# Hybrid decoder step: operand making for the block products spread over steps and slots, a second plain set, decode columns in pairs, squares over PSUM

## The chip, the cores and the metric

The kernel runs on one core of a Trainium2 chip. The metric is the device time of one execution in microseconds (us). Before is the kernel as it stood, after is the changed one.

## The reference

The program is one inference step of a two-layer decoder with a prompt of 1024 tokens and 8 decode tokens, model width 1024, all in float32. Layer 0 is retention (4 heads, keys 256 wide, values 512 wide, chunks of 128 tokens), layer 1 is attention over a sliding window of 128. What matters here is layer 0, cut to its core:

```
h = rmsnorm(x, g_norm);  q, k, v, gate = split(h @ w_in)
# for each chunk c and head:
inner = (q_c @ k_c.T) * dmask
o_c   = inner @ v_c + (q_c @ S) * cross_decay
S     = S * chunk_decay + (k_c * k_decay).T @ v_c
# then:
o = rmsnorm(o, g_out) * silu(gate)
x1 = x + o @ w_out            # 2048 x 1024: "retention's projection"
```

Layer 1 starts with rmsnorm(x1), so the sums of squares of x1 (acc) are wanted too.

## The kernel before

**Split operands.** Every large matmul is made of float32 numbers split in two: hi is the number rounded (a cast, mostly on ACT), lo is what is left (a subtraction on DVE or POOL), and hi.hi + hi.lo + lo.hi are three matmuls. So each operand costs a cast and a subtraction before PE can use it.

**Block products.** The projections use a Winograd form: a 2x2 by 2x2 block product in seven products instead of eight (SEQ7, L316): A11.B11, S2.T2, S1.T1, A12.B21, S3.T3, S4.B22, A22.T4. A and S are weights and their sums, B and T are the data (heads and token parities) and its differences. `XH[t][x]`, `XL[t][x]` are the cells in which hi and lo of operand x lie, for each half t of the tokens; the cells are in the tiles SA and SB. T1 = B12 - B11, T2 = B22 - T1, T3 = T2 - B11, T4 = B21 - T2. Each cell has 256 columns of prompt tokens and 2 of decode tokens (`dec_cols`).

**The steps.** After the input projection come 32 steps of the recurrence, two heads in turn, first heads 0 and 1, then 2 and 3. In step i PE does `b_qk` of step i+1 (scores and the transposes of k), `b_mm` of step i (state S and output po), and `b_tr` of step i-1 (the transposes tr of the normed output on). The function `others` (L1057) gives the order on the other engines: og of step i-2 (DVE, L1055: tr times gate), Sh (ACT) and Sl (DVE, L1023), the sum of squares (ACT) with its scaling ts (DVE, L1034), the power pw on POOL (rsq, L119), the conversions of step i+1 (CONV, L827: sT, qh, vh, kh, kl, sh, vl, sl, ql), and on (ACT, L1042) after the first four of these. og is sent by DMA into the cells of heads 0 and 1, or, for heads 2 and 3, to DRAM (osc).

**Operand making in the steps.** Heads 0 and 1 are done halfway. From then on `x_items` (L1073) makes their operands: for each of four blocks (t, and a half c2 of its tokens) four differences on DVE (L1078, `do`) into temporaries `tm` in G0, seven casts on ACT, and seven subtractions (L1083) on POOL or, for each third, on DVE. The items form a list; three, at each fifth step four, are taken per step, and what is left is done at slot 1 of the projection. The first temporary of a block is also that of the next.

**The projection.** Eight sets (PSet, L1112), n = 0 to 7: phase P = n // 4 is heads 0 and 1 or heads 2 and 3, a = n % 4 a quarter of the output columns. A set has 14 slots of 12 matmuls (`p_prod`), or, in the plain form, 8 slots of 24 (`p_plain`, eight plain block products from B11, B21, B12, B22). Sets of phase one store partial sums to DRAM (pscr), which phase two loads and adds. `p_evac` (L1184) takes products out of PSUM, `p_pre` (L1197) adds partial results, `p_fin` (L1234) finishes x1: square into M01 (ACT, L1246) and add to acc (L1247), a store to xscr, and in set 7 the hi and lo of x1 for layer 1. `p_hi`, `p_lo` (L1166), `p_sum` make the weights' operands in tiles w, s1a, s2a, rb, ra.

**Operands of heads 2 and 3** are made during sets 3 to 5 by `split`, `t_sums` (y and z are their temporaries) and `dec_cols`, which overwrite the cells of heads 0 and 1 once these are read for the last time. Set 4 is plain, since it needs no T operands. In set 7 `a_load` and `a_split` (L1344, L1345) bring x1 of the first six column blocks back as the next layer's operand, and `kv_conv` splits weights of layer 1.

**What sets the order.** PE, ACT, DVE, POOL and SP all work through their own queue in program order, and that order is written by hand: `later(n, fn)` puts fn behind slot n, `when(time, fn)` puts it at a planned time, `others` and the items are put after each step. `p_plan` lists all of it for the sets. An engine that waits at the head of its queue holds everything behind it.

The lines that the prediction speaks of: L991 to L1004 `b_mm`, L104 transposes, L119 power, L300 `dec_on` (on of the decode tokens), L813 vl, L819 qh, L825 ql, L969 and L970 `dec_cols`, L1042 on, L1055 og, L1078 differences and casts of x_items, L1083 their subtractions, L1166 `p_lo`, L1195 evacuations, L1229 transposes of x, L1321 subtractions of `split`, L334 to L336 the matmuls of a product.

Of the kernel before, what the change touches and what calls it, by code (L numbers as in the profile page):

```python
# [70 lines left out]
def _trunk(ctx, tc, nc, a):  # L71
# [743 lines left out]
    def b_qh(h, c):  # L815
        d = heads[h]
        if c > 0:
            d["qh", c] = qt[0][h % 2]
            dve.tensor_copy(d["qh", c], d["l", c][0][:, 0:2, :])  # L819
# [220 lines left out]
    def b_on(h, c):  # L1040
        d = heads[h]
        act(d["on", c], d.pop(("po", c)), AF.Copy, scale=d["ss", c])  # L1042
# [28 lines left out]
    def x_items(t, c2):  # L1071
        cs = slice(128 * c2, 128 * c2 + 128)
        r = {x: raw_of(x, t)[:, :, cs] for x in (B11, B21, B22, T1)}  # L1073
        tm = [G0[:, 512 * j:512 * j + 512].rearrange("p (k f) -> p k f", k=4) for j in range(3)]
        its = []

        def do(fn, *a):
            its.append(lambda: fn(*a))  # L1078

        def parts(x, src):  # L1080
            n = len(its)
            do(act, XH[t][x][:, :, cs], src, AF.Copy)
            do(lambda: (pool if n % 3 else dve).tensor_tensor(XL[t][x][:, :, cs], src, XH[t][x].bitcast(F32)[:, :, cs], SUB))  # L1083
# [113 lines left out]
    def p_pre(s, t):  # L1197
        pool.tensor_tensor(s.c["w"][:, t], s.c["w"][:, t], s.c["x"][:, t], ADD)
# [35 lines left out]
    acc_on = set()  # L1234

    def p_fin(s, key, t):
        i, par = KEY[key]
        ft = 2 * s.a + i
        x1 = s.c[key][:, t, 0:256].rearrange("p (c y) -> p c y", c=2)
        gk = gcol[:, 16 + ft:17 + ft]  # L1240
        if s.n == 7:
            act(toks(A_hi[:, ft], t, par), x1, AF.Copy, scale=gk)
            dve.scalar_tensor_tensor(toks(A_lo[:, ft], t, par), x1, gk, toks(A_hif[:, ft], t, par), MUL, SUB)
        if (par, t) in acc_on:
            sq = M01[:, 0:256].rearrange("p (c y) -> p c y", c=2)
            act(sq, x1, AF.Square)  # L1246
            (pool if s.n == 7 else dve).tensor_tensor(toks(acc, t, par), toks(acc, t, par), sq, ADD)  # L1247
# [30 lines left out]
    def p_plain(s, par, i, t):  # L1278
# [18 lines left out]
        later(n + 1, p_fin, s, key, t)  # L1297
# [20 lines left out]
    def part(x, t, h, src, eng):  # L1318
        hi, lo = cells(x, t, h)
        act(hi, src, AF.Copy)  # L1320
        eng.tensor_tensor(lo, src, hi.bitcast(F32), SUB)  # L1321
# [1015 lines left out]
```

## Time and profile before

| what | us |
|---|---|
| median of 3 runs (1357.2 to 1361.32) | 1357.76 |
| profiled execution | 1358.83 |
| its span | 1357.0 |
| steps 5 to 31 of the recurrence | 560.09 to 702.49 |
| sets 0 to 7 of the projection | 702.49 to 917.30 |
| set 4, the plain one | 799.40 to 828.35 |

The times of the stages are from the start of the span, cut where PE starts each set's first matmul. Of a group of instructions the profile gives the line, engine, operation, tiles out<-in with shapes and count, then busy us and mean ns of one, then the idle time of the engine just ahead of them and what ended it. PE is busy 94% of the span, but a PE that is busy at a granted clock of 0.5 does half the work, so the clock has to be read beside it.

### The profile page before, as it was taken

The page shows a single profiled execution, that of the slowest core. Times are in us where ns is not written, and L with a number is a line of the kernel's source. Part 1 is how long each engine was busy: PE and PEld are TensorE (multiplying, and loading weights), DVE is VectorE, ACT ScalarE, POOL GpSimd, SP SyncE. Part 2 cuts the span into 40 slices and gives each one's busy share as a digit, 9 for nine tenths or more (in the row PEclk, how much of TensorE's full clock was granted, in tenths as well). Part 3 has the DMA queues.
Part 4 walks back from the last instruction along what each step waited for, and adds up shares of the span by engine and source line. Part 5 has one row for each costly group of instructions (what it writes and reads, how often), then busy time and mean ns, then how long its engine had stood idle before and what let it go on. Part 6 is the DMA issues. An engine that isn't in the chain of part 4 may idle for free.

```text
span 1357.0 us, 26895 instructions
## 1 busy us (share of the span) xinstructions
PE 1277.7 (94%) x9743; PEld 1216.5 (90%) x9743; DVE 822.9 (61%) x1590; ACT 693.6 (51%) x1664; POOL 812.6 (60%) x994
## 2 busy tenths in 40 slices
PE   6999999999999999888888986979998999999998
PEld 6999999999999999767778986879998999998998
DVE  6944656565666753688755589764565666766321
ACT  5532544545455644777761243355566666656221
POOL 6753534445389997687865667866567675645000
PEclk9999999999999999999999997989999999999999
DMA  6314677677757744768646672553113120218332
GB/s 220 103 63 151 212 241 214 200 214 204 248 162 230 218 147 139 216 187 264 214 142 173 183 267 88 140 160 105 55 52 101 40 86 32 95 47 270 95 95 80
DMA packets 230322, 208.79 MB, mean 154 GB/s; under 512 B 32889, under 2 KB 206197, under 8 KB 230173
## 3 DMA queue, kind: packets, MB, share of 16 engines
q1 hardware_dynamic: 198192, 172.71, 42.4%
q10 hardware_dynamic: 31996, 34.36, 7.8%
q8 instruction: 77, 1.26, 0.4%
q14 instruction: 57, 0.46, 0.1%
HBM read 134.36 MB, written 69.50 MB: 150 GB/s over the span
## 4 chain that ended last, share of the span: by engine, by line
PE 70%; DVE 8%; POOL 7%; ACT 5%; issue 5%; DMA 4%; SPq 1%; ACTq 0%; DVEq 0%; POOLq 0%
PE b L334 7%; PE b L335 7%; PE b L336 7%; PE pj L1607 5%; PE pj L1608 5%; PE pj L1609 5%; PE b L327 4%; PE b L328 4%; PE b L329 4%; PE tr L104 3%; PE b L543 2%; PE S L336 2%; PE S L334 1%; PE S L335 1%; PE o L1970 1%
## 5 line engine op out<-in xcount | busy, mean ns | idle before, releaser
L334 PE MATMUL b<-xh,woh 128*128 128x258 f32 x784 | 223.2, 285 | 0.0
L336 PE MATMUL b<-xh,wol 128*128 128x258 f32 x784 | 221.7, 283 | 0.0
L335 PE MATMUL b<-xl,woh 128*128 128x258 f32 x784 | 221.6, 283 | 0.0
L1607 PE MATMUL pj<-SA,wh 128*128 128x384 f32 (+1 forms) x512 | 174.7, 341 | 2.3 <-ACT SA L1990 1.3
L1608 PE MATMUL pj<-SA,wh 128*128 128x384 f32 (+1 forms) x512 | 164.3, 321 | 0.2 <-DVE SA L1991 0.2
L1609 PE MATMUL pj<-SA,wl 128*128 128x384 f32 (+1 forms) x512 | 164.5, 321 | 0.0
L334 PEld LDWEIGHTS b<-xh,woh 128*128 128x128 f32 x784 | 148.0, 189 | 4.1 <-issue 3.7
L335 PEld LDWEIGHTS b<-xl,woh 128*128 128x128 f32 x784 | 148.7, 190 | 0.0
L336 PEld LDWEIGHTS b<-xh,wol 128*128 128x128 f32 x784 | 148.0, 189 | 0.0
L225 POOL TENSOR_TENSOR wol<-raw,woh 128x512 fp32r<-128x512 f32 x52 | 68.0, 1318 | 119.7 <-ACT woh L220 108.6
L327 PE MATMUL b<-woh,xh 128*128 128x256 f32 x448 | 126.6, 283 | 0.0
L328 PE MATMUL b<-wol,xh 128*128 128x256 f32 x448 | 126.0, 281 | 0.0
L329 PE MATMUL b<-woh,xl 128*128 128x256 f32 x448 | 125.6, 280 | 0.0
L1607 PEld LDWEIGHTS pj<-SA,wh 128*128 128x128 f32 x512 | 96.7, 189 | 6.5 <-issue 2.6
L1608 PEld LDWEIGHTS pj<-SA,wh 128*128 128x128 f32 x512 | 96.9, 189 | 0.4 <-DVE SA L1991 0.4
L1609 PEld LDWEIGHTS pj<-SA,wl 128*128 128x128 f32 x512 | 96.5, 188 | 0.0
L1948 POOL TENSOR_TENSOR s<-s,sm 128x512 f32<-128x512 f32 x64 | 66.6, 1040 | 48.9 <-DVE sm L1947 44.6
L327 PEld LDWEIGHTS b<-woh,xh 128*128 128x128 f32 x448 | 84.3, 188 | 5.0 <-issue 2.9
L329 PEld LDWEIGHTS b<-woh,xl 128*128 128x128 f32 x448 | 84.3, 188 | 0.0
L328 PEld LDWEIGHTS b<-wol,xh 128*128 128x128 f32 x448 | 84.3, 188 | 0.0
L1940 ACT ACTIVATE s<-s,mx 128x257 f32<-128x257 f32 x128 | 64.2, 505 | 38.2 <-DVE mx L1938 37.3
L220 ACT ACTIVATE woh<-s 128x512 fp32r<-128x512 f32 x88 | 54.1, 624 | 53.3 <-POOL s L210 20.6
(544 smaller groups left out, 3927.3 us busy)
## 6 DMA issues: line engine op xcount, KB each, us to landing
raw<-in_w_in_ret_dram ACTq DMA_DIRECT2D x44, 512.0 KB
st<-in_state_ret_dram SPq DMA_DIRECT2D x64, 256.0 KB
out_dram<-st SPq DMA_DIRECT2D x64, 256.0 KB
vb<-vscr SPq DMA_DIRECT2D x64, 128.0 KB
evp<-qks SPq DMA_DIRECT2D x32, 256.0 KB
evx<-vsc SPq DMA_DIRECT2D x32, 256.0 KB
wr<-in_w_in_swa_dram SPq DMA_DIRECT2D x32, 256.0 KB
evc<-gsc SPq DMA_DIRECT2D x16, 256.0 KB
```

Source lines behind the costliest of these rows:

```text
L225: eng.tensor_tensor(lo, src_of(s, name, sub), hi.bitcast(F32), SUB)
L327: mm(dst, xh, wh, start=a and i == 0, stop=False, skip_group_check=True)
L328: mm(dst, xh, wl, start=False, stop=False, skip_group_check=True)
L329: mm(dst, xl, wh, start=False, stop=z, skip_group_check=True)
L334: mm(dst, wh, xh, start=a, stop=False, **sg)
L335: mm(dst, wh, xl, start=False, stop=False, **sg)
L336: mm(dst, wl, xh, start=False, stop=z, **sg)
L1607: mm(ps, hi[:, k, fs], xh[:, k, t0:t1], start=first and k == ks[0], stop=False)
L1608: mm(ps, hi[:, k, fs], xl[:, k, t0:t1], start=False, stop=False)
L1609: mm(ps, lo[:, k, fs], xh[:, k, t0:t1], start=False, stop=last and k == ks[-1])
L1940: nc.scalar.activation(st[:, j, :], st[:, j, :], AF.Exp, bias=mx[:, j:j + 1], accum_out=sm[:, j:j + 1])
L1948: nc.gpsimd.tensor_tensor(st[:, :, 0:256], st[:, :, 0:256], sm.unsqueeze(2).broadcast_to([128, 2, 256]), ALU.mult)
```

## The change

- **Steps.** qh moves from DVE to ACT, on from ACT to DVE. on now stands behind the first three conversions (sT, qh, vh) instead of four.
- **Operand making in the steps** follows a fixed table: blocks start at steps 6, 12, 18, 25; differences on DVE at +0, +1, +2, +4 of a block; casts on ACT one a step at +0 to +6; all subtractions on POOL, one a step, two steps after their cast. The three temporaries rotate from block to block. What falls past step 31 goes to slots 1 and on.
- **Decode columns**: one cast on ACT and, a step or slot later, one subtraction on POOL, for both t at once, where there were two casts and two subtractions on DVE.
- **Sets**: sets 4 and 5 are plain (before, set 4). The T sums of heads 2 and 3 are staged in three slots each, at four places over sets 4 and 5; T4 is split in set 5 and T3 in set 6. Each split casts in one slot and subtracts in the next.
- **p_fin** comes in two parts, one and two slots behind its product; the square is over both t in one ACT operation into a PSUM tile (tr's pool) and is added to acc by one DVE operation. **p_pre** is done for both t at once. Copies of decode columns go from POOL to ACT. a_split subtracts one slot after it casts.

```diff
@@ steps
-            dve.tensor_copy(d["qh", c], d["l", c][0][:, 0:2, :])
+            act(d["qh", c], d["l", c][0][:, 0:2, :], AF.Copy)
...
-        act(d["on", c], d.pop(("po", c)), AF.Copy, scale=d["ss", c])
+        dve.tensor_scalar(d["on", c], d.pop(("po", c)), d["ss", c], None, MUL)
...
-                      [(b_on, i - 1)] + conv[4:]):
+                      [(b_on, i - 1)] + conv[3:]):
@@ dec_cols
-        dve.tensor_copy(h, src)
-        dve.tensor_tensor(XL[t][x][:, :, 256:258], src, h.bitcast(F32), SUB)
+        if part == 0:
+            act(h, src, AF.Copy)
+        else:
+            pool.tensor_tensor(l_, src, h.bitcast(F32), SUB)
@@ x_items
-            do(act, XH[t][x][:, :, cs], src, AF.Copy)
-            do(lambda: (pool if n % 3 else dve).tensor_tensor(XL[t][x][:, :, cs], src, XH[t][x].bitcast(F32)[:, :, cs], SUB))
+        for i, o_, x, y in ((0, ta, r[T1], r[B11]), (1, tb, r[B22], ta), (2, tc_, tb, r[B11]), (4, ta, r[B21], tb)):
+            put(i, dve.tensor_tensor, o_, x, y, SUB)
+        for i, x in enumerate((B22, T1, T2, B11, T3, B21, T4)):
+            put(i, act, XH[t][x][:, :, cs], src[x], AF.Copy)
+            put(i + 2, pool.tensor_tensor, XL[t][x][:, :, cs], src[x], XH[t][x].bitcast(F32)[:, :, cs], SUB)
@@ psets
-        s.n, s.P, s.a, s.kind, s.fw, s.plain = n, n // 4, n % 4, "p", 128, n == 4
+        s.n, s.P, s.a, s.kind, s.fw, s.plain = n, n // 4, n % 4, "p", 128, n in (4, 5)
@@ p_pre
-        pool.tensor_tensor(s.c["w"][:, t], s.c["w"][:, t], s.c["x"][:, t], ADD)
+        pool.tensor_tensor(s.c["w"], s.c["w"], s.c["x"], ADD)
@@ p_fin
-            act(sq, x1, AF.Square)
-            (pool if s.n == 7 else dve).tensor_tensor(toks(acc, t, par), toks(acc, t, par), sq, ADD)
+                    o_ = s.r["q" + key] = trp.tile([128, 512], F32, name="tr").rearrange("p (t c y) -> p t c y", t=2, c=2)
+                act(o_, x1, AF.Square)
...
+                dve.tensor_tensor(toks2(acc, par), toks2(acc, par), s.r["q" + key], ADD)
@@ p_prod
-        if j == 2:
-            later(n + 1 if s.n else n + 3, p_pre, s, t)
+        if j == 2 and t:
+            later(n + 1 if s.n else n + 3, p_pre, s)
@@ p_plan
-            for h in range(2):
-                L(m + 2 + 2 * t + h, t_sums, t, h)
-            for x in (T1, T2):
-                L(m + 6, lambda x=x, t=t: dec_cols(pq["dT"], 8, x, t))
-            L(q + 1 + 2 * t, lambda t=t: split(T3, t, ST[0][t]))
-            L(q + 5 + 2 * t, lambda t=t: split(T4, t, ST[1][t]))
+            split(m2 + 3 + 2 * t, T4, t, 1)
+            split(q + 1 + 2 * t, T3, t, 0)
+        for k in range(4):
+            t_sums((m + 3, m + 5, m + 7, m2 + 1)[k], k // 2, k % 2, k)
...
-            L(u + 4 + k, a_split, k)
+            later(u + 4 + k, a_split, k, 0)
+            later(u + 5 + k, a_split, k, 1)
```

How the queues move, at three places. First DVE in a step of the recurrence in which a block of operands is started (G is G0 with the temporaries, SA a cell; before):

```order
L1055 TENSOR_TENSOR og<-tr,evw 128x512
L1023 SCALAR_TENSOR_TENSOR Sl<-S,Sh 128x512 x2
L1034 TENSOR_SCALAR bss<-bss,M_88 128x1
L793 TENSOR_TENSOR sT<-tr,M_88 128x128
L819 CAST qh<-evp 128x256
L788 SCALAR_TENSOR_TENSOR kl<-tr,M_88,kh 128x256
L1078 TENSOR_TENSOR G_7435<-G_7435,SA 128x512
```

The same in after:

```order
L1062 TENSOR_TENSOR og<-tr,evw 128x512
L1030 SCALAR_TENSOR_TENSOR Sl<-S,Sh 128x512 x2
L1041 TENSOR_SCALAR bss<-bss,M_88 128x1
L793 TENSOR_TENSOR sT<-tr,M_88 128x128
L1049 TENSOR_SCALAR on<-po,bss 128x512
L788 SCALAR_TENSOR_TENSOR kl<-tr,M_88,kh 128x256
L1549 TENSOR_TENSOR G_7435<-SB,G_7435 128x512
```

The cast of qh has left, and on stands in its place, ahead of kl and of the differences.

Second, DVE where the last T operands of heads 2 and 3 are made, in before at the end of set 4 and the start of set 5 (s1a, s2a and G hold the sums, SA is a cell, evx and evw are output tiles, w and rb belong to set 5's weights):

```order
L1332 TENSOR_TENSOR s1a<-SA,s2a 128x512
L1321 TENSOR_TENSOR SA<-s2a,SA 128x2x256
L1335 TENSOR_TENSOR G_7435<-s1a,G_7435 128x512
L1295 TENSOR_TENSOR evx<-S,evx 128x258
L969 CAST SA<-dT 128x4x2
L970 TENSOR_TENSOR SA<-dT,SA 128x4x2
L969 CAST SA<-dT 128x4x2
L970 TENSOR_TENSOR SA<-dT,SA 128x4x2
L969 CAST SA<-dT 128x4x2
L970 TENSOR_TENSOR SA<-dT,SA 128x4x2
L969 CAST SA<-dT 128x4x2
L970 TENSOR_TENSOR SA<-dT,SA 128x4x2
```

In after, in set 5, which is plain:

```order
L1343 TENSOR_TENSOR s2a<-SA,G_7435 128x512
L1344 TENSOR_TENSOR s1a<-SA,s2a 128x512
L1299 TENSOR_TENSOR evc<-S,evc 128x258
L1252 TENSOR_TENSOR acc<-acc,tr 128x4x128
L1299 TENSOR_TENSOR evp<-S,evp 128x258
L1327 TENSOR_TENSOR SA<-s2a,SA 128x2x256
L1356 TENSOR_TENSOR G_7435<-s1a,G_7435 128x512
L1299 TENSOR_TENSOR evp<-S,evp 128x258
```

The eight small operations are gone from DVE, evacuations stand between the parts of a T sum, and the joined adds to acc appear.

Third, POOL around p_pre, in before in a set of phase one (evw, evx, evp are the partial results, rx and rp the terms to be added, ra and rb raw weights):

```order
L1198 TENSOR_TENSOR evw<-evw,evx 128x258
L1200 TENSOR_TENSOR evx<-evx,rx 128x258
L1200 TENSOR_TENSOR evp<-evp,rp 128x258
L1198 TENSOR_TENSOR evw<-evw,evx 128x258
L1200 TENSOR_TENSOR evx<-evx,rx 128x258
L1200 TENSOR_TENSOR evp<-evp,rp 128x258
L1145 TENSOR_TENSOR s1b<-rb 128x512
L1166 TENSOR_TENSOR w_9530<-ra,w_9530 128x512
```

In after:

```order
L1159 TENSOR_TENSOR w_9512<-ra,w_9512 128x512
L1147 TENSOR_TENSOR s2a<-ra,s2a 128x512
L1191 TENSOR_TENSOR evw<-evw,evx 128x516
L1193 TENSOR_TENSOR evx<-evx,rx 128x516
L1193 TENSOR_TENSOR evp<-evp,rp 128x516
L1138 TENSOR_TENSOR s1b<-rb 128x512
L1159 TENSOR_TENSOR w_9514<-ra,w_9514 128x512
```

Three operations of twice the width stand where six stood, and the subtraction for w behind them is the one of the next operand (A22).

More of the change, by code (lines that the diff above doesn't have):

```diff
@@ L1273, in p_prod @@
             if s.P:
-                later(n + 1, p_fin, s, key, t)
+                p_fins(s, key, t, n)
             elif t:
@@ L1296, in p_plain @@
         later(n + 1, out)
[L1297 removed]
+        p_fins(s, key, t, n)
     def o_load(dst, h, par, t):
@@ new lines, in split, with step, t_sums, b @@
+    def split(k, x, t, src=None, engs=None):
+        def step(lo):
+            v = raw_of(x, t) if src is None else ST[src][t]
+            for h in range(2):
+                piece(x, t, h, hv(v, h), (engs or (dve, pool))[h] if lo else None)
+        later(k, step, False)
+        later(k + 1, step, True)
+    def t_sums(k, t, h, n):
+        def b():
+            return [v.rearrange("p (k n) -> p k n", k=2) for v in pq["yz"][n % 2]] + [hv(ST[0][t], h), hv(ST[1][t], h)]
+        def one():
+            y, z, b11, b21 = b()
+            dve.tensor_tensor(y, hv(raw_of(T1, t), h), b11, SUB)
+            dve.tensor_tensor(z, hv(raw_of(T2, t), h), y, SUB)
+        def two():
+            y, z, b11, b21 = b()
+            piece(T1, t, h, y)
+            piece(T2, t, h, z)
+            pool.tensor_tensor(b21, b21, z, SUB)
+        def three():
+            y, z, b11, b21 = b()
+            piece(T1, t, h, y, dve)
+            piece(T2, t, h, z, pool)
+            dve.tensor_tensor(b11, z, b11, SUB)
+        for n_, fn in enumerate((one, two, three)):
+            later(k + n_, fn)
@@ new lines, in p_plan, with DC @@
+        q = psets[6].n0
+        def DC(k, x, plain=False):
+            later(k, lambda: dec_cols(pq["dT"], 8, x, 0, plain))
+            later(k + 1, lambda: dec_cols(pq["dT"], 8, x, 1, plain))
+        later(n, st_open)
+        later(n, lambda: dec_sums(pq["dT"], 8))
+        for t in range(2):
+            split(n + 3 + t, B11, t, 0)
+            split(n + 8 + t, B21, t, 1)
+            later(n + 9 + t, o_load, raw_of(T3, t)[:, :, 0:256], 0, 1, t)
+            later(n + 11 + t, o_load, raw_of(B22, t)[:, :, 0:256], 1, 1, t)
+            later(m, o_load, raw_of(T1, t)[:, :, 0:256], 0, 1, t)
+            later(m, o_load, raw_of(T2, t)[:, :, 0:256], 1, 1, t)
+            split((n + 13, m)[t], T3, t)
+            split(m + 1 + t, B22, t)
+            split(m2 + 3 + 2 * t, T4, t, 1)
+            split(q + 1 + 2 * t, T3, t, 0)
@@ L1497, in _trunk @@
     nc.sync.dma_start(out=M23, in_=a["c1"][:, 384:640])
-    items = []
+    for q, i0 in enumerate((6, 12, 18, 25)):
+        x_items(q, i0)
+    for n, x in enumerate((B11, T2, T1, B21, T3, B22, T4)):
+        for part in range(2):
+            items.setdefault(9 + n + part, []).append((dec_cols, (dT, 0, x, part)))
     xdg = x_decode()
@@ L1516, in _trunk @@
             dec_gate()
-        for _ in range(4 if i % 5 == 0 else 3):
-            if items:
-                items.pop(0)()
-        if i in (5, 9, 13, 17):
-            items += x_items((i - 5) // 8, (i - 5) // 4 % 2)
+        for fn, args in items.pop(i, ()):
+            fn(*args)
         if i in (20, 23, 26, 29, 31):
             p_early((20, 23, 26, 29, 31).index(i))
-    print("left", len(items))
     p_plan()
@@ L1536, in _trunk @@
             p_open()
+            for i in sorted(items):
+                later(1 + i - NS, lambda its: [fn(*args) for fn, args in its], items[i])
         for fn, args in (at.pop(n, ()) if n else ()):
```

138 lines of the change are left out of this document (56 added, 82 removed).

## The prediction

> **What bounds the kernel now.** I read the page first (span, and the chain that ended last), then the table of stretches cut where the stages begin on TensorE, then what PE waited for in the stretch that the change touches.
>
> ```profile
> span 1357.0 us, 26895 instructions
> PE 70%; DVE 8%; POOL 7%; ACT 5%; issue 5%; DMA 4%; SPq 1%; ACTq 0%; DVEq 0%; POOLq 0%
> ```
>
> PE carries 70% of the chain; DVE, POOL and ACT together 20%. A gain here comes from PE's waits, not from less work on any other engine. The stretches below are the recurrence (from step 5), set 0, sets 1 and 2, then sets 3, 4, 5, 6, 7; columns are the stretch and its length, busy us of PE, PEld, DVE, ACT, POOL with counts, the granted clock, the DMA share and GB/s. The ninth and tenth rows cut out two stretches at half clock.
>
> ```profile
> 560.09:702.49 142.40, 126.17 (x655) 101.67 (x653) 108.92 (x232) 105.55 (x242) 107.90 (x129) 0.98 0.68 212
> 702.49:731.64 29.15, 23.21 (x175) 22.41 (x174) 13.50 (x33) 7.56 (x16) 16.46 (x23) 0.94 0.60 148
> 731.64:772.29 40.65, 40.65 (x338) 40.44 (x337) 24.74 (x55) 10.49 (x19) 27.72 (x36) 1.00 0.60 165
> 772.29:799.40 27.11, 22.24 (x170) 21.82 (x169) 18.93 (x33) 9.75 (x19) 15.86 (x15) 0.94 0.72 237
> 799.40:828.35 28.95, 23.37 (x194) 23.16 (x192) 26.25 (x36) 11.94 (x22) 20.30 (x17) 0.97 0.66 213
> 828.35:861.98 33.63, 25.43 (x168) 24.75 (x169) 28.35 (x48) 13.09 (x27) 25.63 (x30) 0.77 0.36 107
> 861.98:882.18 20.20, 20.20 (x171) 20.20 (x169) 14.78 (x25) 7.37 (x16) 15.13 (x19) 1.00 0.54 152
> 882.18:917.30 35.12, 25.19 (x171) 24.25 (x169) 21.20 (x32) 17.48 (x31) 23.13 (x28) 0.83 0.48 153
> 673.24:680.07 6.83, 6.10 (x20) 5.23 (x21) 6.06 (x10) 5.65 (x13) 6.83 (x7) 0.50 0.52 163
> 727.90:731.20 3.30, 3.30 (x17) 3.30 (x17) 0.93 (x3) 0.63 (x1) 2.62 (x6) 0.50 0.53 125
> ```
>
> Set 6 has PE busy throughout: 20.20 us is what a product set costs by itself. The plain set has 8 block products in place of 7, so its own time is 20.20 x 8/7 = 23.1. What each stage spends beyond that, its excess: set 0 29.15 - 20.2 = 8.95; sets 1 and 2 40.65 - 40.4 = 0.25; set 3 6.9; set 4 28.95 - 23.1 = 5.85; set 5 13.4; set 6 0; set 7 14.9. Together 50.25 us.
>
> ```profile
> PE tr L104 <- ACT on L1042: 18.3, 18, 2.9
> PE S L336 <- DVE w L1166: 10.7, 3, 5.2
> PE S L334 <- DVE evw L1195: 8.2, 4, 6.0
> PE S L336 <- POOL w L1166: 6.7, 4, 2.3
> PE S L334 <- ACT w L1161: 5.6, 1, 5.6
> ```
>
> These are PE's waits from 555 to 925 (total, times, longest). In the recurrence all of it is one wait: the transposes of on, 18 times, 18.3 us. With half of the 6.10 busy us at clock 0.50 (3.05) its excess is 21.35. **All excess: 71.6 us.** That is what the change can play for. The profiled execution took 1358.83 us, 1.07 above the median of 1357.76, so a gain counted in one is taken off the other unchanged.
>
> **The steps.** Two step starts without a wait between give PE's pace:
>
> ```profile
> 627.76 0.48 PE L991 MATMUL S<-vh,kh 128*128 128x512 f32 x1
> 632.34 0.47 PE L991 MATMUL S<-vh,kh 128*128 128x512 f32 x1
> ```
>
> 4.58 us. The other engines in the same steps (groups of the stretch from 560; L300 is from the whole kernel; the two rows of stretches are those of lines L1083 and, after it, L1078):
>
> ```profile
> L1042 ACT ACTIVATE on<-po,bss 128x512 f32<-128x512 f32 x27 | 18.5, 687 | 6.2 <-POOL bss L119 5.2
> L300 DVE TENSOR_SCALAR evc<-od,oss 128x512 f32<-128x512 f32 x4 | 3.0, 748 | 1.2 <-POOL oss L119 1.2
> L819 DVE CAST qh<-evp 128x256 fp32r<-128x256 f32 x24 | 11.1, 464 | 0.0
> L813 POOL TENSOR_TENSOR vl<-evx,vh 128x512 fp32r<-128x512 f32 x26 | 33.9, 1303 | 3.5 <-ACT vh L808 2.8 <-POOL bss L119 0.6
> L825 POOL TENSOR_TENSOR ql<-evp,qh 128x256 fp32r<-128x256 f32 x25 | 21.6, 865 | 0.0
> L1083 POOL TENSOR_TENSOR SA<-G,SA 128x512 fp32r<-128x512 f32 x8 | 9.5, 1197 | 0.0
> 560.09:702.49 142.40, 7.54 (x9) 21.12 (x17) 0.98 0.68 212
> 560.09:702.49 142.40, 17.13 (x16) 16.49 (x28) 0.98 0.68 212
> ```
>
> Per step (27 of them by the count of on) ACT is busy 105.55/27 = 3.9, DVE 4.0, POOL 4.0 us, all under 4.58. So no engine paces the steps; single steps do, in which the table of operand work falls badly. One of them, with the wait of 2.18 at its end:
>
> ```profile
> 579.27 1.76 DVE L1078 TENSOR_TENSOR G<-G,SA 128x512 f32<-128x512 f32 x1
> 579.13 1.34 POOL L813 TENSOR_TENSOR vl<-evx,vh 128x512 fp32r<-128x512 f32 x1
> 599.02 0.69 DVE L1078 TENSOR_TENSOR G<-SA 128x512 f32<-128x512 f32 x1 [2.96 <-POOL SB L1083]
> 603.21 0.66 PE L104 MATMUL tr<-ident,on 128*128 128x128 f32 x4 [2.18 <-ACT on L1042]
> ```
>
> DVE stands 2.96 us before a new block's first sum, because POOL still reads the temporary of the block before; behind it stand og, Sl and the sum of squares, then POOL's power, ACT's on and PE. The change takes this wait away: the temporaries rotate, and a block starts six steps after the last one. A remainder: the DVE lo's, 9 in 7.54 us, go to POOL; qh (0.46) goes to ACT and on comes to DVE at about 0.75 (the L300 row; ACT's is 0.69). DVE: 4.0 - 0.46 - 0.28 + 0.75 = 4.0. ACT: 3.9 - 0.69 + qh, between half a 128x512 cast (16.49/28 = 0.59) and a whole one, taken as 0.4: 3.6. POOL gains 9 or 10 lo's at 1.2 and seven pairs of decode columns at, I estimate, 0.2 to 1.0 (a 128x8 subtraction, next to the L970 below): 10 x 1.2 + 7 x 0.5 = 15.5 over 27 steps, 4.0 + 0.6 = 4.6. This is the term with no cover left: PE's step is 4.58.
>
> Against it stands what the first two timeline rows show: a DVE sum of two SBUF operands that starts beside a POOL operation takes 1.76, alone 0.69. With qh and the lo's off DVE, only 16 sums are left there that can meet POOL so, and ql should fall from 0.865 towards 0.6 to 0.75 (a half and more of the 1.2 that a 128x512 takes on POOL), vl from 1.30 towards 1.2. That gives back 0.2 to 0.35 a step: POOL 4.3 to 4.4. [...]
>
> So the steps' excess: from 21.35 to **8** (4, if no wait over 1 us is left, to 14, if POOL's blocks of seven steps each run some 0.3 over); gain 13.4.
>
> **Set 0.** Excess 8.95 today.
>
> ```profile
> 716.58 0.45 DVE L1229 STREAM_TRANSPOSE evw<-xr 128x256 f32<-128x256 f32 x1 [6.24 <-DMA xr<-in_x_prompt_dram]
> 726.03 1.29 POOL L1166 TENSOR_TENSOR w<-ra,w 128x512 fp32r<-128x512 f32 x1
> L1198 POOL TENSOR_TENSOR evw<-evw,evx 128x258 f32<-128x258 f32 x4 | 4.0, 998 | 3.2 <-DVE evx L1192 3.2
> ```
>
> The transposes' wait for x is untouched. The last tr of the steps shortens (part of 18.3). But p_pre, joined over both t, is three operations of 516 columns ahead of A22's lo; each costs POOL between 1.2 (a 128x512) and 2.0 (two of 0.998), and all of it now comes after the second t: 1 to 3 us later than now. And two operand groups of steps 32 and 33 are flushed in here. I take **9** (6 to 12). Sets 1 and 2: **0.5**.
>
> **Sets 3 to 5.** Set 3's excess of 6.9 began with DVE standing 3.25 us in front of a lo whose cast on ACT, in the same slot, waited for a load; behind it the decode columns:
>
> ```profile
> 782.45 0.69 DVE L1321 TENSOR_TENSOR SA<-G,SA 128x512 fp32r<-128x512 f32 x1 [3.25 <-ACT SA L1320]
> 772.29:861.98 89.69, 11.77 (x16) 0.89 0.57 180
> 772.29:861.98 89.69, 10.04 (x16) 0.89 0.57 180
> L1247 DVE TENSOR_TENSOR acc<-acc,M 128x256 f32<-128x256 f32 x9 | 5.6, 617 | 4.8 <-ACT M L1246 4.8
> ```
>
> Rows two and three are the columns' casts (L969) and subtractions (L970): 32 operations on a few elements hold DVE for 21.8 us of its 18.93 + 26.25 + 28.35 = 73.5, and in set 4 DVE is busy 91%, in set 5 84%. They leave DVE for ACT and POOL as 16 operations. The squares' nine adds of 0.617 become one of 128x512 per pair with a PSUM operand (0.75, as L300), and ACT's square goes from two of about 0.42 to one of 0.6 to 0.84. DVE's lo now comes one slot (1.43) after the cast. So DVE has 73.5 - 21.8 - 2 = some 50 us of work in sets of 20.2 + 23.1 + 23.1 = 66. Set 3: **1.5** (0 to 4). Set 4: **1** (0 to 3); the waits of 5.6 and 5.2 (ACT's and DVE's w of set 5, behind the T sums and eight column operations) lose their cause, since set 5 as a plain set needs no T operand. Set 5 pays 23.1 - 20.2 = **2.9** for it, and **1** (0 to 4) on top. POOL, busy 15.86 + 20.30 + 25.63 = 61.8 now, gets the columns (8 x 0.5) and loses with set 5 four S sums at about 1.2 and six p_pre operations at about 1.0, and two lo's to set 6: 61.8 + 4 - 4.8 - 6 - 2.4 = 52.6 of 66, 80%, still room. Excess here from 26.15 to 6.4.
>
> Set 6 takes over the T3 split and is now the first to use the T operands of heads 2 and 3: **1.5** (0 to 4; at worst one more wait of the POOL row's 2.3 with its half clock).
>
> **Set 7.** Excess 14.9; the largest wait is 6.0, for evw behind this row:
>
> ```profile
> 907.06 2.20 DVE L1345 SCALAR_TENSOR_TENSOR SA<-SA,gcol 128x1024 fp32r<-128x1024 f32 x1 [0.86 <-ACT SA L1344]
> ```
>
> DVE waits for ACT's half of a_split in the same slot; one slot later it won't, and squares over PSUM shorten what it does. kv_conv on POOL stays. I take **8** (4 to 12).
>
> **Half clock.** After a wait of at most 2.3 us (the POOL row) the clock was 0.50 from 727.90 to 731.20, which cost half of its 3.30: a wait of 2 can cost 3.7. My remainders hold such pieces, about three. [...]
>
> **Sum.** After: 8 + 9 + 0.5 + 1.5 + 1 + 2.9 + 1 + 1.5 + 8 = 33.4; gain 71.6 - 33.4 = 38.2. Profiled 1358.8 - 38.2 = 1320.6; median 1357.76 - 38.2 = **1319.6**. All low ends give 4 + 6 + 0 + 0 + 0 + 2.9 + 0 + 0 + 4 = 16.9, a gain of 54.7 (1303); all high ends 14 + 12 + 0.5 + 4 + 3 + 2.9 + 4 + 4 + 12 = 56.4, a gain of 15.2 (1342.5).
>
> **Rivals.** (A) POOL becomes the pace of the steps. Its 4.6 without relief is over 4.58, and the power for the next step queues behind it. The steps keep their 21.35; only the sets gain: 38.2 - 13.4 = 24.8, so 1333. For it: POOL's load; against: ql and sT were slowed by what leaves. 15%. (B) The change removes waits in name only: on, now on DVE, stands behind Sl and in front of kl, so each late power now also holds DVE, and tr waits as often for DVE; in the sets the loads (DMA share 0.72 in set 3) land late whoever waits. Excess stays near 70: 1356. 4%. (C) Slower: POOL paces the steps at slowed durations. [...] The mean step today is 142.4/27 = 5.27. [...] 6%, as POOL's mean of 4.0 is far from it.
>
> Forecast 75%, A 15%, B 4%, C 6%. The range takes the forecast's ends and A: 1304 to 1342. About 0.3%, 4 us, is what a measurement of this kernel can tell from no change: faster 0.90, same 0.04, slower 0.06.
>
> **What would show it.** Right: step starts 4.6 apart with PE's wait at tr under 6 us in all; no L969-like small operation on DVE; set 4 near 24, set 5 near 24, set 6 near 21.5, set 7 near 28; no clock of 0.50 between 827 and 861 of today. Wrong: POOL busy over 95% from step 8 on (A, C), tr waiting for DVE's on in most steps (B), set 0 over 33, or set 7 still at 35.

## The result, and the profile after

The changed kernel takes 1326.41 us (median of 4 runs, 1321.99 to 1328.74), 0.976 of before (95% interval 0.9728 to 0.9791): about 31 us faster where 38.2 were forecast, and inside the range of 1304 to 1342. The profiled execution took 1328.74 us, its span is 1326.9. In the same stretches as in the prediction (first steps 0 to 4 of before, which the prediction did not look at, then after's steps 0 to 4, steps 5 to 31, set 0, sets 1 and 2, and sets 3 to 7; set 7 to its last matmul):

```profile
537.14:560.09 22.95, 20.06 (x109) 16.67 (x110) 11.57 (x28) 15.45 (x35) 15.70 (x25) 1.00 0.67 196
```

```profile
537.20:564.10 26.90, 22.14 (x109) 18.25 (x110) 13.16 (x28) 13.81 (x35) 15.43 (x25) 0.87 0.55 167
564.10:696.45 132.35, 123.02 (x655) 101.33 (x653) 100.84 (x203) 99.42 (x248) 118.77 (x145) 0.99 0.74 229
696.45:725.15 28.70, 23.63 (x176) 23.04 (x175) 13.21 (x32) 7.12 (x21) 16.34 (x13) 0.90 0.63 162
725.15:765.98 40.83, 40.83 (x338) 40.83 (x338) 21.46 (x50) 10.73 (x26) 25.50 (x22) 0.99 0.57 155
765.98:791.53 25.55, 22.29 (x171) 21.86 (x169) 14.65 (x24) 10.95 (x22) 16.76 (x15) 0.93 0.82 271
791.53:814.73 23.20, 23.20 (x195) 23.20 (x194) 17.51 (x24) 10.09 (x24) 16.39 (x14) 1.00 0.85 271
814.73:837.93 23.20, 23.20 (x195) 23.20 (x194) 18.04 (x26) 9.26 (x21) 14.49 (x11) 1.00 0.48 141
837.93:858.23 20.30, 20.30 (x170) 20.23 (x169) 12.98 (x22) 9.15 (x21) 14.25 (x11) 1.00 0.46 144
858.23:886.28 28.05, 23.73 (x170) 23.13 (x168) 22.85 (x28) 16.17 (x28) 17.66 (x11) 0.88 0.53 180
```

Sets 4, 5 and 6 are full: PE is busy throughout at clock 1.00. The two sets that held the largest waits, 4 and 5, give 28.95 - 23.20 = 5.75 and 33.63 - 23.20 = 10.43 us. Against the forecast:

| stage | gain forecast | gain measured |
|---|---|---|
| steps 0 to 4 | not in the sum | -3.95 |
| steps 5 to 31 | 13.4 | 10.05 |
| set 0 | 0 | 0.45 |
| sets 1 and 2 | -0.25 | -0.18 |
| set 3 | 5.4 | 1.56 |
| set 4 | 4.85 | 5.75 |
| set 5 | 9.5 | 10.43 |
| set 6 | -1.5 | -0.10 |
| set 7 | 6.9 | 5.6 |
| the rest | 0 | 0.5 |

The sets together gave 23.5 of 24.8; in that sum set 3 fell 3.8 short, and sets 4 to 6 made up 3.2 of it. The steps gave 6.1 (10.05 - 3.95) of 13.4. In the row of set 7 both kernels are taken to the set's last matmul (before: 33.67). PE's waits in after, from 530 to 900:

```profile
PE tr L104 <- DVE on L1049: 11.4, 9, 3.0
PE S L336 <- POOL w L1159: 7.8, 3, 3.2
PE S L334 <- DVE evw L1188: 3.2, 2, 2.2
PE tr L776 <- issue: 2.3, 1, 2.3
PE S L336 <- DVE w L1159: 1.7, 2, 0.9
```

Three places hold most of it: on, with waits up to 3.0; the subtraction for w on POOL, three times; and evw, mostly in set 7 (2.24).

**A wait that was said to be gone.** What after's table puts at step 20, on POOL and DVE, and PE behind it (one fence each):

```profile
640.01 1.21 POOL L1549 TENSOR_TENSOR SB<-G,SB 128x512 fp32r<-128x512 f32 x1
641.16 1.31 POOL L1549 TENSOR_TENSOR SB<-SB 128x512 fp32r<-128x512 f32 x1
```

```profile
641.25 1.76 DVE L1549 TENSOR_TENSOR G<-G,SA 128x512 f32<-128x512 f32 x1 [2.38 <-POOL SB L1549]
```

```profile
646.56 0.63 PE L104 MATMUL tr<-ident,on 128*128 128x128 f32 x4 [3.02 <-DVE on L1049]
```

DVE stands 2.38 us before a difference, as it did in before, then takes 1.76 beside POOL's next operation, and PE waits 3.02 for on. The temporaries do rotate, but T3 of a block, its third difference, is written to the temporary that holds T4 of the block before, whose subtraction stands at the same step (6 + 2 = 8 steps after that block's start). The old wait came at a block's first difference; the new one comes at its third. It occurs in steps 14 and 20; the fourth block starts seven steps after the third and escapes it.

**A wait that no stretch of the prediction held.** ACT in step 1 of after:

```profile
545.91 0.42 ACT L819 ACTIVATE qh<-evp 128x256 fp32r<-128x256 f32 x1 [5.66 <-DMA gsc<-raw]
546.75 0.46 ACT L783 ACTIVATE kh<-tr,M 128x256 fp32r<-128x256 f32 x1
```

The profile puts ACT's wait at qh, 5.66 us, down to gsc<-raw, the last stores of the input projection, issued from 540.24 to 541.73; vh, kh, Sh and PE's next step (549.10) stand behind. It was not the load of q, as the expectations of runs 3 and 4 have it: PE read the tile with q at 539.36 (tr<-evp). Probably qh is written where raw lay; no run shows that. In before DVE waited there, for 1.33 us, with kl and og behind it, and ACT went on:

```profile
544.67 0.58 DVE L819 CAST qh<-evp 128x256 fp32r<-128x256 f32 x1 [1.33 <-DMA gsc<-raw]
```

**The joined p_pre** in set 3, on POOL:

```profile
780.77 1.68 POOL L1191 TENSOR_TENSOR evw<-evw,evx 128x516 f32<-128x516 f32 x1 [0.33 <-DVE evx L1185]
782.53 1.31 POOL L1193 TENSOR_TENSOR evx<-evx,rx 128x516 f32<-128x516 f32 x1
783.79 1.74 POOL L1193 TENSOR_TENSOR evp<-evp,rp 128x516 f32<-128x516 f32 x1
785.49 1.73 POOL L1159 TENSOR_TENSOR w<-rb,w 128x512 fp32r<-128x512 f32 x1
```

A22's subtraction for w starts only at 785.49; PE waits 2.45 us for it, until 787.28, and the clock behind it is 0.50 until 790.7 (0.93 over the set): matmuls start 0.215 us apart there, 0.12 at 1.00.

### The profile page after: what moved, and what is told of

It reads as the page before. It is cut to its first block, busy times and chain, and to the rows that moved or that the text cites. A ratio compares the mean times of both kernels' runs of the same rounds, so it can differ in the third digit from the quotient of the medians.

```text
span 1326.9 us, 26895 instructions
## 1 busy us (share of the span) xinstructions
PE 1275.2 (96%) x9767; PEld 1217.6 (92%) x9767; DVE 790.1 (60%) x1511; ACT 682.7 (51%) x1686; POOL 797.9 (60%) x935
## 4 chain that ended last, share of the span: by engine, by line
PE 78%; POOL 6%; DVE 5%; issue 4%; DMA 4%; ACT 2%; SPq 1%; POOLq 0%; ACTq 0%; DVEq 0%
PE b L334 8%; PE b L335 7%; PE b L336 7%; PE pj L1634 6%; PE pj L1635 5%; PE pj L1636 5%; PE b L327 4%; PE b L328 4%; PE b L329 4%; PE S L1293 3%; PE tr L104 3%; PE o L1997 2%; PE b L543 2%; PE S L336 1%; PE S L334 1%
```

## The experiments

Each was timed beside runs of the kernel before (1359.93 to 1361.12 us there), so ratios to before are compared; after's is 0.976 (0.9728 to 0.9791). Stage lengths are those of the profiled executions.

**1. T3's difference one step later.**

```diff
-(2, tc_, tb, r[B11])
+(3, tc_, tb, r[B11])
```

> After with one number changed: a block's third difference (T3's) is put at its fourth step in place of its third. Theory: the reuse of a temporary was not removed but moved. T3 of a block goes into the temporary of T4 of the block before, whose subtraction POOL makes in the same step, and DVE stands 2.4 us before it at two steps. Then DVE's two waits of 2.4 go, PE's waits at tr of 2.0 and 3.0 us and one piece of half clock (1.5) go with them, and the 32 steps fall from 159.25 to about 153; the whole by some 6 us to about 1320. Rival: POOL paces these two steps, since two subtractions of two blocks fall in them; then the two steps stay over 6 us and the steps over 157.

1322.21 us, 0.9728 (0.9706 to 0.975). Its steps 5 to 31, and the difference that waited:

```profile
563.26:690.68 127.42, 121.20 (x654) 100.11 (x653) 99.64 (x203) 99.65 (x248) 119.14 (x145) 1.00 0.76 238
642.43 0.70 DVE L1549 TENSOR_TENSOR G<-G,SA 128x512 f32<-128x512 f32 x1
```

The wait is gone, the difference takes 0.70, and the steps fall from 132.35 to 127.42: 4.9 us, with the half clock behind the wait (in after 0.50 from 647.6 to 650.8, here 1.00 over the stretch). Nearly all of it is behind the second of the two waits: steps 21 and 22 together fall from 13.88 to 9.69 us, steps 15 to 17, behind the first, only from 14.40 to 14.27. POOL does the same work in the same steps (119.14 us), so it was not POOL's load that made them long in after. What is left may be another matter. From step 8 on, where the subtractions begin, POOL is busy here for 97% of the time:

```profile
577.76:690.68 112.92, 107.08 (x579) 88.52 (x578) 88.03 (x178) 88.83 (x221) 109.97 (x133) 1.00 0.75 234
```

No run took the blocks' subtractions off POOL, so whether it paces the rest is not shown.

**2. The exchange of qh and on undone.**

```diff
-            act(d["qh", c], d["l", c][0][:, 0:2, :], AF.Copy)
+            dve.tensor_copy(d["qh", c], d["l", c][0][:, 0:2, :])
-        dve.tensor_scalar(d["on", c], d.pop(("po", c)), d["ss", c], None, MUL)
+        act(d["on", c], d.pop(("po", c)), AF.Copy, scale=d["ss", c])
-conv[0:3] + [(b_on, i - 1)] + conv[3:]
+conv[0:4] + [(b_on, i - 1)] + conv[4:]
```

> After with the exchange of engines undone: qh on DVE and on on ACT, in before's order; operand items and sets as after. Theory: the table of items is what gained in the steps, the exchange gives little: steps 1 and 2 get 4 us back, and from step 5 on the waits at tr grow by 2 to 5 us; the whole within 3 us of after. Rival: the exchange carries the gain in the steps: from step 5 on the stretch to set 0 goes from 132.3 back to 138 or more, the whole 3 to 6 us slower than after.

0.9751 (0.9728 to 0.9774), the same as after. Steps 5 to 31:

```profile
563.09:696.37 133.28, 124.43 (x655) 102.84 (x653) 99.58 (x199) 107.03 (x250) 119.63 (x145) 0.97 0.74 227
```

133.28 against 132.35: the exchange is worth at most 0.9 us there, less than the 2 to 5 that were expected. The gain of the steps is the table's. Step 1 took 7.6 us (after 9.15), step 2 6.46 (after 5.88), in part at half clock (0.50 from 545 to 549, 0.67 from 549 to 553): 1.0 of the expected 4 us came back.

**3. qh on DVE for the first chunks of heads 0 and 1 alone.**

```diff
+            if c == 1 and h < 2:
+                dve.tensor_copy(d["qh", c], d["l", c][0][:, 0:2, :])
+            else:
+                act(d["qh", c], d["l", c][0][:, 0:2, :], AF.Copy)
```

> After with the cast of qh back on DVE in one place alone, the first chunks of heads 0 and 1; later casts stay on ACT. Theory: in step 1 q's load lands late; on ACT the cast holds vh, kh and Sh behind it, on DVE it held only kl. Steps 1 and 2, 9.15 and 5.88 us in after against 6.52 and 4.57 before, go back to about 6.5 and 4.6, and the whole falls by about 4 us. Rival: the load itself came later in the profiled execution (its cast began 1.2 us later than before), and any engine would wait: steps 1 and 2 stay over 14 us together.

0.9748 (0.9727 to 0.9768). Step 1 took 8.52 us and step 2 6.03: by its numbers the rival. But the run tells less than it was meant to. In after's order on stands behind qh on DVE too, and with the wait there, PE's longest wait at tr was 4.2. It showed that the place behind the waiting cast matters, not the engine alone; run 4 was made for that.

**4. T3 later, p_pre for each t (run 5), and qh behind vh and kh on ACT.**

```diff
-    CONV = (b_sT, b_qh, b_vh, b_kh, b_kl, b_sh, b_vl, b_sl, b_ql)
+    CONV = (b_sT, b_vh, b_kh, b_qh, b_kl, b_sh, b_vl, b_sl, b_ql)
```

> After with T3's difference later, p_pre for each t, and in the steps the cast of qh behind those of vh and kh on ACT. Theory: in step 1 ACT stood at qh, whose load landed late, and kh, Sh and all behind it waited; with qh third, step 1 goes from 8.7 to 6.5 to 7.6 as where qh was on DVE, and the whole falls by 1.5 to 3 us against the run with the two repairs (1319.66). Rival: the load holds PE itself, since the products with q can't start either; step 1 stays over 8.3.

1316.99 us, 0.9672 (0.9659 to 0.9684). ACT in step 1:

```profile
544.21 0.47 ACT L783 ACTIVATE kh<-tr,M 128x256 fp32r<-128x256 f32 x1 [2.19 <-DVE sT L793]
545.84 0.42 ACT L819 ACTIVATE qh<-evp 128x256 fp32r<-128x256 f32 x1 [1.15 <-DMA gsc<-raw]
```

The wait ends at 545.84, but kh is done by then, and step 1 takes 6.58 us. But counted from the start of the step the cast began at 5.16 us here and at 5.97 in after, so the order is not the only difference. Two executions in which it ended alike are those of run 7, with this order, and run 11, with qh first on ACT (one fence each):

```profile
545.05 0.42 ACT L819 ACTIVATE qh<-evp 128x256 fp32r<-128x256 f32 x1 [1.33 <-DMA gsc<-raw]
```

```profile
545.11 0.42 ACT L819 ACTIVATE qh<-evp 128x256 fp32r<-128x256 f32 x1 [4.97 <-DMA gsc<-raw]
```

That is 5.34 (run 7) and 5.28 us (run 11) into step 1, which took 5.90 and 8.46 us: with the wait ending alike, the order is worth 2.5 us (run 12, with qh first too: 5.26 and 8.44). Over all the profiled executions step 1 took 8.4 to 9.2 with qh first on ACT, 6.5 to 7.6 with qh on DVE and on on ACT, 5.9 and 6.6 with qh third.

**5. p_pre for each t again.**

```diff
-    def p_pre(s):
+    def p_pre(s, t):
...
-        if j == 2 and t:
-            later(n + 1 if s.n else n + 3, p_pre, s)
+        if j == 2:
+            later(n + 1 if s.n else n + 3, p_pre, s, t)
```

> After with p_pre again for each t by itself, as before the change; all else as after. Theory: joining it is what sets 0, 3 and 7 still wait for: three operations of 1.3 to 1.7 us stand in one piece ahead of A22's subtraction on POOL, and PE waits 3.25, 2.45 and 2.08 us for it, with a stretch of half clock each time. Split, these waits fall to 1.4 or less, sets 0, 3 and 7 together from 82.3 to about 75, and the whole by about 7 us. Rival: POOL's total work ahead of A22 decides, six operations at 0.7 to 1.0 take as long as three, and the three sets stay within 2 us of 82.

1324.54 us, 0.9739 (0.9718 to 0.9761), by the whole time not told from after. Sets 0, 1, 3 and 7:

```profile
698.97:724.44 25.47, 22.75 (x176) 22.33 (x174) 11.76 (x25) 6.50 (x20) 16.70 (x16) 0.93 0.65 166
724.44:746.75 22.31, 20.69 (x171) 20.30 (x170) 13.38 (x32) 5.74 (x14) 12.73 (x12) 1.00 0.66 167
766.94:791.10 24.16, 20.64 (x171) 20.31 (x169) 12.56 (x24) 10.94 (x22) 15.55 (x16) 1.00 0.85 285
858.02:883.66 25.64, 21.23 (x170) 20.37 (x168) 21.00 (x27) 15.80 (x27) 19.19 (x14) 1.00 0.57 196
```

Sets 0, 3 and 7 fall from 82.3 to 75.3, the number that was expected; set 1 pays 1.7 of it back (22.31 for 20.62). But the reason that was expected holds in set 0 alone, where PE's wait for POOL's w fell from 3.25 to 0.84 us. In set 7 it was 2.08 us and is now in two, 1.72 and 0.35; in set 3 it grew from 2.45 to 3.52, because a subtraction of a split (1.65 us) now stands between the two pieces on POOL, and A22's starts at 786.56. PE behind it, here and in run 6 (one fence each):

```profile
788.35 0.39 PE L336 MATMUL S<-SB,w 128*128 128x258 f32 x1 [3.52 <-POOL w L1159]
```

```profile
780.34 0.58 PE L336 MATMUL S<-SB,w 128*128 128x258 f32 x1 [3.52 <-POOL w L1159]
```

The wait is the same, but in run 5 the clock over the set was 1.00, the first matmul behind the wait took 0.39 and set 3 24.16 us; in run 6 these were 0.93, 0.58 and 26.18. So the 1.4 us that set 3 gained in run 5 is luck. Over the profiled executions with A22 on POOL it took 24.2 to 24.3 us at a mean clock of 1.00 and 25.2 to 26.2 at 0.93, with p_pre joined or split. Sets 0, 1 and 7 differ each time (joined: after and runs 1, 2, 3, 11 and, but for set 7, 12; split: runs 4, 5 and 6): set 0 takes 27.4 to 29.5 joined and 24.5 to 25.5 split, set 7 27.4 to 28.2 and 25.6 to 26.0, and set 1 20.2 to 20.6 and 22.1 to 22.4, the other way. How the splitting acts in set 7, where the wait for w is not shorter, is not shown.

**6. Both repairs: T3 later and p_pre for each t.**

> After with both repairs: T3's difference one step later, and p_pre for each t by itself. Theory: the two act in different stages and add: steps as in the run with T3 later (153), sets 0, 1, 3 and 7 together as in the run with p_pre split (97.6 against 102.9), the whole 6 to 9 us under after, near 1319. Rival: with the steps shorter, set 0 starts earlier and waits for its loads instead (x comes by a load of its own); then set 0 is back near 28 and the whole is no better than 1322.

1319.66 us, 0.9696 (0.9679 to 0.9713). Steps 5 to 31 took 127.18, set 0 24.96: they add in these stages. Set 3 took 26.18, over after's 25.55, with the wait of 3.52 and a mean clock of 0.93; sets 0, 1, 3 and 7 took 99.5, not the 97.6 that were expected.

**7. And A22's subtraction on DVE in sets 0 to 3 and 6, on top of run 4.**

```diff
-eng = eng or (pool if name in ("A12", "A22") else dve)
+eng = eng or (pool if name == "A12" or name == "A22" and (s.plain or s.n == 7) else dve)
```

> The same, and A22's subtraction on DVE in place of POOL in the product sets 0, 1, 2, 3 and 6. Theory: PE's waits for POOL's w are for A22's subtraction behind p_pre; on DVE, which has room in these sets, they go, and sets 0, 1 and 3, together 73.5 in the run with the two repairs, fall to 66 to 70. Rival: DVE is held by its own evacuations and by waits for loads in the same sets, and the waits come back as DVE's: the three sets stay over 71.5.

1315.31 us (1312.33 to 1317.84), 0.9663 (0.965 to 0.9677): the fastest kernel, though its interval overlaps that of run 4. Sets 0, 3 and 4:

```profile
687.41:710.32 22.91, 21.20 (x175) 20.81 (x174) 12.79 (x26) 6.47 (x20) 15.88 (x15) 1.00 0.68 176
752.48:774.87 22.39, 20.74 (x171) 20.32 (x169) 12.80 (x22) 8.66 (x18) 11.76 (x12) 1.00 0.79 265
774.87:801.14 26.27, 23.45 (x194) 23.25 (x193) 19.70 (x28) 12.36 (x28) 20.41 (x18) 1.00 0.90 288
```

Sets 0, 1 and 3 take 67.2 us (72.8 in run 4), and the wait of 3.52 in set 3 is gone, so DVE had the room. Set 4, full in after, now waits once for POOL's w (2.8 us): perhaps an earlier set 4 meets work that used to be done, but no run shows it.

**8. Before with the second plain set alone**, the splits of T3 and T4 moved to set 6.

```diff
-s.plain = ..., n == 4
+s.plain = ..., n in (4, 5)
-            L(q + 1 + 2 * t, lambda t=t: split(T3, t, ST[0][t]))
-            L(q + 5 + 2 * t, lambda t=t: split(T4, t, ST[1][t]))
+            L(q6 + 1 + 2 * t, lambda t=t: split(T3, t, ST[0][t]))
+            L(q6 + 5 + 2 * t, lambda t=t: split(T4, t, ST[1][t]))
```

> Before with one part of the change: set 5 is plain too, and the splits of T3 and T4 of heads 2 and 3 stand at the same slots of set 6 in place of set 5; columns, T sums and squares as before. Theory: the waits of 5.6 and 5.2 us at set 5's start were for T operands that came too late, and a plain set doesn't ask for them: set 5 goes from 33.6 to 23 to 25, set 6 from 20.2 to at most 23, the whole 6 to 10 us faster than before. Rival: DVE's queue (91% busy in set 4) is what was late, and it delays set 5's evacuations and weights as well: set 5 stays over 27 and the whole within 4 us of before.

0.9983 (0.9971 to 0.9996), about nothing. Set 5, set 6, ACT and PE at set 5's start:

```profile
828.47:857.09 28.62, 25.85 (x193) 25.56 (x194) 16.66 (x31) 7.21 (x16) 9.35 (x16) 0.86 0.45 134
857.09:884.36 27.27, 22.81 (x170) 22.43 (x169) 22.78 (x35) 11.22 (x23) 20.38 (x23) 0.87 0.36 107
```

```profile
825.56 0.63 ACT L1320 ACTIVATE SA<-s2a 128x512 fp32r<-128x512 f32 x1 [0.83 <-DVE s2a L1331]
827.23 0.63 ACT L1320 ACTIVATE SA<-s1a 128x512 fp32r<-128x512 f32 x1 [1.04 <-DVE s1a L1332]
827.77 1.22 ACT L1161 ACTIVATE w<-rb 128x512 fp32r<-128x512 f32 x2
```

```profile
828.47 2.09 PE L1289 MATMUL S<-SA,w 128*128 128x258 f32 x8 [5.70 <-ACT w L1161]
```

The wait of 5.70 is still there, in a plain set that needs no T operand. It was for set 5's first weights: their cast stands on ACT behind the casts of the T sums, and these wait for DVE (s2a, s1a). What set 5 saves, 5.0, set 6 loses, 7.1. These are the rival's numbers: set 5 over 27, the whole within 4 us of before.

**9. Before with the decode columns on ACT and POOL.**

```diff
-        dve.tensor_copy(h, src)
-        dve.tensor_tensor(XL[t][x][:, :, 256:258], src, h.bitcast(F32), SUB)
+        act(h, src, AF.Copy)
+        pool.tensor_tensor(XL[t][x][:, :, 256:258], src, h.bitcast(F32), SUB)
```

> Before with one part of the change: the casts of the decode columns go from DVE to ACT and their subtractions to POOL, not joined into pairs. Theory: 32 small operations that hold DVE for 21.8 us in sets 3 to 5 are the cause of DVE's lateness there; sets 3 to 5 together go from 89.7 to 80 to 84, DVE's busy time there from 73.5 to about 52. Rival: the T sums and the waits of DVE on casts in the same slot set the pace, and POOL's queue gets what DVE loses: sets 3 to 5 stay over 86.

0.9946 (0.9929 to 0.9964). Sets 3 to 5:

```profile
768.79:857.12 88.33, 71.14 (x530) 69.90 (x529) 56.37 (x87) 37.25 (x85) 67.37 (x77) 0.87 0.61 194
```

DVE's busy time fell from 73.53 to 56.37, and the sets from 89.69 to 88.33 only: the rival's numbers. Of the 0.5%, 3.7 us came in steps 5 to 31 (138.70).

**10. Before with staged splits and T sums.** Each `split` casts in slot k and subtracts in k + 1; each `t_sums` is done in slots k, k + 1, k + 2, from the slots of before.

> Before with one part of the change: every split of heads 2 and 3 casts in one slot and subtracts in the next, and every T sum is done in three slots, from the same slots as before; one plain set, columns on DVE as before. Theory: what was late in sets 3 to 5 were ACT and DVE standing in front of each other's operations of the same slot; staged, sets 3 to 5 go from 89.7 to 77 to 82 with no second plain set, and the whole 8 to 12 us under before. Rival: staging needs the room of the second plain set; with one, the T operands come later than before and set 5 waits for them: sets 3 to 5 stay over 86.

0.9955 (0.9941 to 0.9969). Sets 3 to 5:

```profile
773.06:861.67 88.61, 70.13 (x531) 68.86 (x530) 72.87 (x117) 33.45 (x67) 61.04 (x60) 0.89 0.58 184
```

Set 3 (24.75) and set 4 (25.53) gain, together 5.8 us; set 5 (38.33) loses 4.7, with one wait of 8.0 for DVE's w. The expectation's theory is wrong for staging alone, and its rival's number came.

**11. After with the columns' pairs on DVE.**

```diff
-            act(h, src, AF.Copy)
+            dve.tensor_copy(h, src)
-            pool.tensor_tensor(l_, src, h.bitcast(F32), SUB)
+            dve.tensor_tensor(l_, src, h.bitcast(F32), SUB)
```

> After with the decode columns' pairs back on DVE, cast and subtraction, at the same places. Theory: in the new staging DVE has room for 16 small operations; sets 3 to 5 stay within 2 us of after's 71.95 and the steps within 2 of 159.25, the whole within 3 us of after. Rival: the columns' engine is what the gain in these sets comes from: sets 3 to 5 grow by 5 us or more.

0.9738 (0.9718 to 0.9757), the same as after; sets 3 to 5 take 71.13 (after 71.95).

**12. After with the staging undone**: both halves of a split, all parts of a T sum, and both halves of a_split in one slot.

```diff
-        later(k + 1, step, True)
+        later(k, step, True)
-            later(k + n_, fn)
+            later(k, fn)
-            later(u + 5 + k, a_split, k, 1)
+            later(u + 4 + k, a_split, k, 1)
```

> After with the staging undone: a split's subtraction in the slot of its cast, the three parts of a T sum in one slot, a_split's two halves in one slot; two plain sets, columns on ACT and POOL, squares over PSUM as after. Theory: sets 3 to 5 grow from 71.95 by 4 to 9 us, set 7 from 28.05 by 2 to 5; the whole 6 to 14 us over after. Rival: the second plain set and the columns together already gave DVE and ACT the room, and staging adds nothing: sets 3 to 5 within 2 us of 72, set 7 within 1 of 28.

1335.14 us, 0.9808 (0.9796 to 0.9821). Sets 3 to 5, then set 7, and DVE and PE in set 7:

```profile
766.67:839.09 72.42, 68.68 (x554) 68.26 (x553) 50.62 (x72) 31.11 (x66) 48.40 (x38) 0.98 0.73 228
859.49:892.60 33.11, 22.50 (x170) 21.55 (x168) 21.55 (x27) 16.01 (x27) 16.81 (x11) 0.90 0.46 156
```

```profile
884.71 1.28 DVE L1369 SCALAR_TENSOR_TENSOR SA<-SA,gcol 128x1024 fp32r<-128x1024 f32 x1 [2.23 <-ACT SA L1367]
```

```profile
887.47 0.55 PE L334 MATMUL S<-SB,w 128*128 128x258 f32 x1 [7.31 <-DVE evw L1188]
```

Sets 3 to 5 stay at 72: there the staging is worth 0.5 us and not the expected 4 to 9. Set 7 goes from 28.05 to 33.11, nearly before's 33.67: there it is all of the gain, and DVE again waits for ACT's half of the same slot, with evw behind.

## Why the prediction was right or wrong, step by step

- **The steps' pace: the outcome right, the sum in part by luck.** POOL came to 118.77/27 = 4.40 us a step, as worked out (4.3 to 4.4), under PE's 4.58. But the relief of 0.2 to 0.35 a step hardly came: ql fell from 0.865 to 0.79, the power from 0.59 to 0.55, vl from 1.30 to 1.29, and the small subtraction on sT rose from 0.61 to 0.69, together some 0.05. With qh's cast back on DVE (run 2) ql took 0.79 and the one on sT 0.68 too, so that cast was not what slowed them. The 4.40 came out because less was added: 13.1 us (nine subtractions, 11.1, and the columns' seven, 2.0) in place of 15.5. And the mean takes in three steps without subtractions. From step 8 on POOL's work is 109.59/24 = 4.57 us a step, as much as PE's: the term with no cover left was just that.
- **The signs.** PE's waits at tr were 11.4 us, not under 6. Sets 4 to 6 came in under the times named, at clock 1.00. POOL was busy for 93% from step 8 on, under the 95% named for rivals A and C, and tr waited for on nine times, not in most steps (B).
- **"The change takes this wait away: the temporaries rotate": wrong.** This is the step that failed. It followed the first temporary and not the third. Run 1 prices it at 4.9 of the missing 7.3 us. With it mended the excess of steps 5 to 31 is 127.42 - 121.05 = 6.4, under the 8 of the forecast. (121.05 is the 142.40 of before less its excess of 21.35.)
- **Steps 0 to 4 were left out: wrong by 3.95.** The exchange was priced as two durations, 0.46 and 0.75. Its other part, which engine stands in the wait for the stores and what is queued behind it there, was not priced. Step 1 lost 2.65 of it, and runs 7 and 11, with that wait ending alike, differ there by 2.5; the rest, 1.3 in step 2, is half clock (0.50 until 551.6), which some executions with before's order show too (6.1 to 6.5 us in step 2 of runs 2, 8 and 10, with a clock of 0.87 to 0.93 over steps 0 to 4; before 1.00).
- **p_pre: right in set 0; set 3 was missed for another reason.** It was priced in set 0 (1 to 3 us later), and there run 5 takes the wait for POOL's w from 3.25 to 0.84 us and the set from 28.70 to 25.47. The 2 us that it is worth in set 7 were not priced. In set 3 the forecast looked at DVE alone and weighed POOL by its load, not by what stands ahead of A22's subtraction: 1.5 of excess was forecast, 25.55 - 20.20 = 5.35 came. Splitting p_pre did not take that wait away (3.52 for 2.45); the subtraction on DVE did (run 7: 22.39, against 26.20 in run 4).
- **Sets 4 and 5: the gain right, the reason wrong.** The forecast gave three causes: no T operand needed in set 5, DVE relieved of 21.8 us, and the subtraction one slot later. Runs 8, 9 and 10 do each alone and get 4.4 (given back in set 6), 1.4 and 1.1 us of the 17.7; runs 11 and 12 take two of them away again, one at a time, and change next to nothing there (71.13 and 72.42 for 71.95). DVE's work in the three sets came to 50.2 us, as worked out (some 50). What is left is the second plain set together with the new places of the operand work: four T sums over both sets, in every other slot, in place of four in a row in set 4, with T4 in set 5 and T3 in set 6; and the squares over PSUM with p_fin in two parts. That it is the places is argued from what the runs leave over, and stays open: no run moved the T sums alone, and none undid the squares.
- **Set 7: right.** The one-slot distance in a_split is worth 5.1 (run 12). The prediction's 14.9 ran up to the next stage's first matmul. To there set 7 takes 29.46 us in after, to its last matmul 28.05: 9.3 of excess stayed, where 8 (4 to 12) were forecast.
- **Half clock: as the prediction took it, but not each time.** It let a wait of 2 us bring half clock. After set 7's wait of 2.08 the clock was 0.50, after a wait of 2.01 in the steps 1.00:

```profile
869.80:872.20 2.40, 2.40 (x13) 2.40 (x13) 2.40 (x3) 0.60 (x2) 2.40 (x2) 0.50 0.55 225
617.60:620.00 2.40, 2.40 (x16) 2.17 (x17) 1.16 (x4) 1.84 (x5) 2.40 (x5) 1.00 0.95 305
```

In run 5 it was 1.00 over set 3 with a wait of 3.52 in it. So in these runs the length of a wait does not settle the clock behind it.
- **The steps' excess: 132.35 - 121.05 = 11.3 where 8 were forecast.** on, with its PSUM operand, took 0.75 on average, as L300 did, while POOL was busy for 90% of the stretch; the mean step took 132.35/27 = 4.90, under before's 5.27, so rival C's slower steps did not come:

```profile
L1049 DVE TENSOR_SCALAR on<-po,bss 128x512 f32<-128x512 f32 x27 | 20.3, 751 | 18.8 <-POOL bss L119 18.7
```

Of the excess 4.9 came from the wait for a buffer (run 1); what makes the other 6.4 is not shown.

## What to carry to other kernels

When buffers rotate, follow every one of them from its last reader to its next writer, not the first alone: the reuse wait had moved two steps on and cost 4.9 us. When an operation moves to another engine, ask what it waits for and what then stands behind it there; its duration was the small part. When one engine's queue is the limit, read what stands ahead of the operation that is waited for, not the engine's load. And where parts of a change are tried alone and each gives little, the gain can still be theirs together: in sets 4 and 5 it may have taken both the room and work moved into it, which the runs leave likely and not shown.
